# Chunk mask as four more features, score products in a row, and a regrouped output projection in a two-layer attention and convolution encoder

## The chip, the cores and the metric

One core of one Trainium2 chip. The metric is the time of one execution on the device, in microseconds (us). It was measured three times before the change.

## What is computed

Two layers work on 512 tokens of 1024 features in float32. Each layer adds half a SwiGLU network, then a mixing block, then half of another SwiGLU network, and normalises. The mixing block is what the change touches:

```python
h  = RMSNorm(x);  p = h @ W_in
# group A: 8 heads of latent attention; a head has 64 + 32 features of q and k, 64 of v
scores = einsum('bhqd,bhkd->bhqk', qs, ks) * scale      # 128 queries at a time
allowed = k_chunk <= q_chunk                            # chunks of 64 tokens
probs = softmax(where(allowed, scores, -1e30));  outs = probs @ vs
# group B: gated 512 channels, causal depthwise convolution over 31 tokens, layer norm, SiLU
x = x + concat(A, B) @ W_out                            # 512 + 512 rows
```

A block of 128 queries sees the keys up to its own end, so the mask matters only in the last 128 keys of a block: there the first 64 queries may not see the last 64 keys.

## The kernel before

Features lie on the 128 partitions and tokens along the free dimension, so an activation of 1024 features is eight blocks of 128 x 512. Large products are made of three fast ones each: operands are split into a high part of reduced precision and a low part that holds the rest, and `mm3` (L152 to L154) adds high x high, high x low and low x high. A weight block is 128 x 1024; `load_w` (L132) fetches it on SP's queue into `raw` (three buffers), ACT casts the high part into `wh` (L136), and the low part `wl` is made in one of three ways: by a subtraction on VectorE, by one on GpSimd (kinds named in `POOLW`; L142), or, for kind "sum", by a negated copy on ACT (L139) and a DMA on GpSimd's queue that adds the source (L140). `wh` and `wl` have four buffers each. PSUM has seven banks for `ps` and one called `cv`.

In `mix_body` the projections come first, in the order of `SEQ`. Queries (L711) and keys (L740) are made with tokens on the partitions, 96 features a head. Then each head runs through five stages, one behind another by the lags in `ORDER`: `turn` transposes q and k (L777, L782) and scales them (L779, L784); `scores` makes four score blocks of 128, 256, 384 and 512 keys (L800, contracted over 96 rows in two float32 passes), adds the mask to each by a bf16 product of `mrow` and `mneg` (L801), takes the largest (L802, VectorE) and the exponential (L806, ACT) of each; `turn_p` transposes the probabilities (L821) and copies them out (L824); `values` multiplies by v (L834); `turn_out` turns every pair of heads back (L852) and splits it (L159, L160) into one of the four blocks `at`. Blocks of 128 and 256 keys share a bank.

Beside the attention the convolution runs in the other engines: two of its four blocks wholly on VectorE (L888), two as products on ACT (L892) and additions on GpSimd (L896), `pr` in three buffers. Its four blocks `ys` are then summed on GpSimd (L910 to L912); a product with `onesm` gives the mean over channels (`pm`, L914); it is subtracted (L920), squares are taken and summed over channels by eight small products (L196), and `spread` (L215) broadcasts the scale. The four blocks `cv` come out of L930, L932 and the split.

The output projection has eight blocks of rows of its output. The weights of the first four (`WOP`) are loaded early, kind "sum", behind the keys; those of the last four when a buffer is free, kind "wo" (GpSimd). Three blocks (`WOG`) have their attention rows (k 0 to 3) multiplied early, between the steps of the convolution's norm; then come their convolution rows, then the next three blocks and the last two. Each result is added to x (L945).

The framework derives the waits between engines from the tiles, and orders each engine's instructions ahead of time with a simulated timeline, by the order in the program and by when operands are ready. Engines run their own instructions in that order. `tc.issue_after(i)` puts the instructions of a block behind instruction i on i's engine.

## Time and profile before

| | |
|---|---|
| three runs, us | 1805.57, 1805.58, 1807.63 |
| median, us | 1805.58 |
| the profiled execution, us | 1805.54 |
| its span in the profile, us | 1803.8 |
| granted TensorE clock | 0.999 |
| data moved | 226.23 MB, mean 125 GB/s |

PE is TensorE's products and PEld its weight loads, DVE is VectorE, POOL is GpSimd, SP issues loads. The span is the profiled execution from its first to its last instruction. In a row of the timeline the first number is the start and the second how long it took until the last of the merged instructions ended; a bracket tells how long the engine stood idle before, and who ended that. Products overlap one another in PE, so that start-to-start distances, not durations, tell what one costs.

### The profile page before, as it was taken

The page shows a single profiled execution, that of the slowest core. Times are in us where ns is not written, and L with a number is a line of the kernel's source. Part 1 is how long each engine was busy: PE and PEld are TensorE (multiplying, and loading weights), DVE is VectorE, ACT ScalarE, POOL GpSimd, SP SyncE. Part 2 cuts the span into 40 slices and gives each one's busy share as a digit, 9 for nine tenths or more (in the row PEclk, how much of TensorE's full clock was granted, in tenths as well). Part 3 has the DMA queues.
Part 4 walks back from the last instruction along what each step waited for, and adds up shares of the span by engine and source line. Part 5 has one row for each costly group of instructions (what it writes and reads, how often), then busy time and mean ns, then how long its engine had stood idle before and what let it go on. Part 6 is the DMA issues. An engine that isn't in the chain of part 4 may idle for free.

```text
span 1803.8 us, 30598 instructions
## 1 busy us (share of the span) xinstructions
PE 1786.7 (99%) x12198; PEld 1645.8 (91%) x12198; DVE 1423.3 (79%) x1975; ACT 1088.8 (60%) x1685; POOL 422.2 (23%) x343
## 2 busy tenths in 40 slices
PE   9999999999999999999999999999999999999998
PEld 7899999888788899999888999998978788999997
DVE  7888887588956979887779888866999668888873
ACT  5565656457953565656635656554779535656564
POOL 1000000258843000000310000002589410000001
PEclk9999999999999999999999999999999999999999
DMA  5657574324102466664326575743250126575742
GB/s 172 165 132 193 123 187 112 108 88 135 31 24 99 126 163 162 151 163 126 123 65 170 122 195 121 194 110 110 80 147 6 52 79 167 129 189 126 187 112 73
DMA packets 70415, 226.23 MB, mean 125 GB/s; under 512 B 7936, under 2 KB 8320, under 8 KB 70272
## 3 DMA queue, kind: packets, MB, share of 16 engines
q1 hardware_dynamic: 54000, 169.74, 28.1%
q0 software_dynamic: 16128, 54.53, 17.7%
q8 instruction: 95, 1.56, 0.4%
q14 instruction: 48, 0.39, 0.1%
q10 hardware_dynamic: 144, 0.00, 0.0%
HBM read 222.15 MB, written 2.10 MB: 124 GB/s over the span
## 4 chain that ended last, share of the span: by engine, by line
PE 80%; DVE 8%; ACT 5%; POOL 3%; issue 3%; DMA 1%; SPq 0%; ACTq 0%; POOLq 0%; DVEq 0%
PE ps L154 26%; PE ps L152 25%; PE ps L153 25%; POOL y L896 2%; PE ps L834 1%; DVE wl L244 1%; ACT pr L892 1%; DVE x L449 1%; DVE r L160 1%; ACT r L806 1%; PE ps L800 1%; DVE wl L142 1%; DVE cv L888 1%; DMA raw<-in_wgu 1%; ACT wh L136 1%
## 5 line engine op out<-in xcount | busy, mean ns | idle before, releaser
L153 PE MATMUL ps<-r,wh 128*128 128x256 f32 (+1 forms) x3436 | 1062.3, 309 | 0.1
L152 PE MATMUL ps<-r,wh 128*128 128x256 f32 (+1 forms) x3436 | 1061.0, 311 | 0.6 <-ACT r L159 0.3
L154 PE MATMUL ps<-r,wl 128*128 128x256 f32 (+1 forms) x2668 | 845.6, 318 | 2.6 <-DVE wl L142 1.2
L152 PEld LDWEIGHTS ps<-r,wh 128*128 128x128 f32 x3436 | 650.9, 190 | 38.6 <-ACT wh L136 2.1
L153 PEld LDWEIGHTS ps<-r,wh 128*128 128x128 f32 x3436 | 652.3, 190 | 36.4 <-issue 2.4
L154 PEld LDWEIGHTS ps<-r,wl 128*128 128x128 f32 x2668 | 506.9, 190 | 41.3 <-DVE wl L142 3.0
L136 ACT CAST wh<-raw 128x1024 fp32r<-128x1024 f32 (+3 forms) x148 | 132.1, 900 | 211.0 <-issue 101.3
L367 POOL DMA_DIRECT2D ls<-in_wgu x72 | 62.5, 869 | 741.7 <-ACT ls L366 615.3
L242 ACT CAST wh<-fr 128x1024 fp32r<-128x1024 f32 (+1 forms) x160 | 157.6, 985 | 101.5 <-DVE fr L387 39.7
L142 DVE TENSOR_TENSOR wl<-raw,wh 128x1024 fp32r<-128x1024 f32 (+3 forms) x132 | 146.8, 1117 | 91.0 <-ACT wh L136 90.0
L154 PE MATMUL ps<-r,ls 128*128 128x256 f32 x768 | 216.7, 282 | 0.0
L244 DVE TENSOR_TENSOR wl<-fr,wh 128x1024 fp32r<-128x1024 f32 (+1 forms) x160 | 182.9, 1143 | 40.3 <-ACT wh L242 40.3
L896 POOL TENSOR_TENSOR y<-y,pr 128x511 f32<-128x511 f32 (+14 forms) x120 | 157.4, 1312 | 54.6 <-ACT pr L892 47.4
L154 PEld LDWEIGHTS ps<-r,ls 128*128 128x128 f32 x768 | 145.2, 189 | 0.0
L244 DVE TENSOR_TENSOR wl<-raw,wh 128x1024 fp32r<-128x1024 f32 (+1 forms) x100 | 113.7, 1137 | 24.6 <-ACT wh L242 24.1
L189 POOL TENSOR_TENSOR r<-r,t 128x512 f32<-128x512 f32 x45 | 77.4, 1728 | 172.7 <-ACT t L185 171.9
L242 ACT CAST wh<-raw 128x1024 fp32r<-128x1024 f32 (+1 forms) x100 | 97.9, 979 | 27.9 <-PE ps L153 19.9
L366 ACT ACTIVATE ls<-fr 128x1024 fp32r<-128x1024 f32 (+1 forms) x56 | 56.1, 1002 | 78.6 <-PE ps L154 65.2
L892 ACT ACTIVATE pr<-r,vec 128x511 f32<-128x511 f32 (+14 forms) x120 | 85.3, 735 | 10.1 <-POOL y L896 10.1
L888 DVE SCALAR_TENSOR_TENSOR cv<-r,vec,cv 128x511 f32<-128x511 f32 (+14 forms) x120 | 88.0, 733 | 3.4 <-ACT cv L884 2.1
L449 DVE SCALAR_TENSOR_TENSOR x<-ps,x 128x512 f32<-128x512 f32 x112 | 77.1, 689 | 15.8 <-PE ps L154 15.4
L367 POOL DMA_DIRECT2D ls<-in_wdq x32 | 27.6, 863 | 260.5 <-ACT ls L366 260.5
(220 smaller groups left out, 2441.5 us busy)
## 6 DMA issues: line engine op xcount, KB each, us to landing
fr<-in_wgu SPq DMA_DIRECT2D x112, 512.0 KB, 3.4
ls<-in_wgu POOLq DMA_DIRECT2D x72, 512.0 KB, 6.3
raw<-in_wgu SPq DMA_DIRECT2D x62, 512.0 KB, 5.0
fr<-in_wdq SPq DMA_DIRECT2D x48, 384.0 KB, 4.6
ls<-in_wdq POOLq DMA_DIRECT2D x32, 384.0 KB, 4.7
raw<-in_wd SPq DMA_DIRECT2D x32, 384.0 KB, 3.1
raw<-in_wd SPq DMA_DIRECT2D x32, 256.0 KB, 2.7
raw<-in_wcv SPq DMA_DIRECT2D x16, 512.0 KB, 3.2
```

Of the source, the lines that this page charges most:

```text
L136: order["cast"] = A.copy(hi[:, :w], raw[:, :w]).ins
L142: (G if kind in POOLW.split() else V).tensor_tensor(lo[:, :w], raw[:, :w], hi[:, :w].bitcast(FP), ALU.subtract)
L152: T.matmul(o, lh, rh, start=first, stop=False, skip_group_check=free)
L153: T.matmul(o, lh, rl, start=False, stop=False, skip_group_check=free)
L154: order["mm"] = T.matmul(o, ll, rh, start=False, stop=last, skip_group_check=free).ins
L242: A.copy(hi[:, :w], src[:, :w])
L244: order["lo"] = V.tensor_tensor(lo[:, :w], src[:, :w], hi[:, :w].bitcast(FP), ALU.subtract).ins
L367: G.dma_start(out=lo[:, :n], in_=w, accum_op=ALU.add)
L449: return V.scalar_tensor_tensor(v, o.rearrange("p (m t) -> p m t", m=2), 0.5 * sign, v, ALU.mult, ALU.add).ins
L888: V.scalar_tensor_tensor(acc[:, s:], u[c][:, :S - s], tap(k), acc[:, s:], ALU.mult, ALU.add)
L892: A.activation(pr[:, s:], u[c][:, :S - s], AF.Copy, scale=tap(k))
L896: order["conv"] = G.tensor_tensor(acc[:, s:], acc[:, s:], pr[:, s:], ALU.add).ins
```

## The change

- q and k of a head get four more features (`DM` = 100). Feature i belongs to the i-th block of 128 tokens. In q it is 1 for the first 64 tokens of that block, in k it is -1e30 for the last 64 tokens; all else is 0. The values stand in 32 new columns of `consts`, and `mask_columns` writes them on GpSimd. The score product adds the mask itself; the products of `mrow` and `mneg` are gone.
- In `scores` the four products of a head are issued first, then the four reductions and exponentials.
- The output projection takes its weights as two blocks of output to one buffer, first (k 0 to 3) or second half (k 4 to 7) of the rows. The first halves of six blocks are loaded, kind "sum", behind the exponentials of heads 0, 2 and 4; their products run early: blocks 0 and 1 with k 0 to 2 ahead of the last `turn_out`, the rest between the steps of the norm. The second halves are loaded with the low part on VectorE; the last two blocks as before, kind "wo".
- The sum over `ys` runs on VectorE, block 2 last. The mean comes from a product with `ones`, and 1/512 goes into a fused subtraction. Mean, sums and scale of the norm use the bank `cv` instead of `ps`.
- Switches that are no longer used are removed.

```diff
+DM = DQ + 4
+WOH = (0, 2, 4)
...
+        def mask_columns(v, o):
+            G.tensor_tensor(v[:, :, :, DQ:DM], cst[:, o:o + 16].rearrange("p (t i) -> p t i", t=NT)[:, :, None, :]
+                            .to_broadcast([P, NT, H, 4]), ones.rearrange("p (t h i) -> p t h i", t=NT, h=H), ALU.mult)
...
-            for i in range(NT):
-                n = (i + 1) * P
-                o = (b01[:, 0:128], b01[:, 128:384], b2[:, 0:384], b3)[i]
-                T.matmul(o, qT[0:DQ, i * P:(i + 1) * P], kT[0:DQ, 0:n], start=True, stop=False)
-                heads[h]["s"] = T.matmul(o[:, n - 64:n], mrow, mneg, start=False, stop=True).ins
+            os = b01[:, 0:128], b01[:, 128:384], b2[:, 0:384], b3
+            for i, o in enumerate(os):
+                heads[h]["s"] = T.matmul(o, qT[0:DM, i * P:(i + 1) * P], kT[0:DM, 0:(i + 1) * P], start=True,
+                                         stop=True).ins
+            for i, (o, p) in enumerate(zip(os, ps)):
                 V.tensor_reduce(mx[:, i:i + 1], o, axis=AX.X, op=ALU.max, negate=True)
...
+        def load_wo(half, m, kind=""):
+            w = load_w(wout[l, m:m + 2, :, half * S:(half + 1) * S].rearrange("m p k -> p m k"), WC, kind, 2)
+            for i in range(2):
+                wo[half, m + i] = [v[:, i * S:(i + 1) * S] for v in w]
+        def products(ms, ks):
+            for k in ks:
+                for m in ms:
+                    if m not in early:
+                        early[m] = bank()
+                    w = wo[k // 4, m]
+                    c = slice(k % 4 * P, (k % 4 + 1) * P)
+                    mm3(early[m], w[0][:, c], w[1][:, c], *(at + cv)[k], k == 0, k == KD - 1)
...
+                if stage is turn_out and h == H - 1:
+                    for m, i in enumerate(WOH):
+                        with tc.issue_after(order["keys"]), tc.issue_after(heads[i]["e"]):
+                            load_wo(0, 2 * m, "sum")
+                    with tc.issue_after(order["values"]):
+                        products((0, 1), range(3))
...
-        with tc.issue_after(order["keys"]):
-            wo = [load_w(wout[l, m], WC, "sum") for m in range(WOP)]
...
+        with tc.issue_after(heads[H - 1]["s"]):
+            products((0, 1), range(3, 4))
         ysum = tmp()
-        G.tensor_tensor(ysum, ys[0], ys[1], ALU.add)
-        G.tensor_tensor(ysum, ysum, ys[2], ALU.add)
-        (G if YP else V).tensor_tensor(ysum, ysum, ys[3], ALU.add)
-        pm = bank()
-        T.matmul(pm, onesm, ysum, start=True, stop=True)
+        for a, b in ((ys[0], ys[1]), (ysum, ys[3]), (ysum, ys[2])):
+            V.tensor_tensor(ysum, a, b, ALU.add)
+        pm = own()
+        T.matmul(pm, ones, ysum, start=True, stop=True)
...
-        early_groups(range(E1, E2))
+        products((2, 3), range(4))
...
-            V.tensor_tensor(ys[c], ys[c], pm, ALU.subtract)
+            V.scalar_tensor_tensor(ys[c], pm, -1.0 / CW, ys[c], ALU.mult, ALU.add)
...
+        r = st.token(CW, own())
+        for m in (0, 2, 4):
+            load_wo(1, m)
+        products((4, 5), range(4))
+        pr = spread(r, own())
...
+        products(range(3), range(4, KD))
+        for m in range(3):
+            add(m)
+        for m in range(3, KD - 2):
+            products((m,), range(4, KD))
+            add(m)
+        ws = [load_w(wout[l, m], WC, "wo") for m in (KD - 2, KD - 1)]
+        for m, w in zip((KD - 2, KD - 1), ws):
+            early[m] = bank()
+            group(early[m], w, at + cv, range(KD), KD)
+            add(m)
```

## The prediction

> **What bounds the kernel now.** I read the page first, then the windows over one attention stage, then PE's timeline there, then its waits.

> ```profile
> span 1803.8 us, 30598 instructions
> PE 1786.7 (99%) x12198; PEld 1645.8 (91%) x12198; DVE 1423.3 (79%) x1975; ACT 1088.8 (60%) x1685; POOL 422.2 (23%) x343
> PEclk9999999999999999999999999999999999999999
> PE 80%; DVE 8%; ACT 5%; POOL 3%; issue 3%; DMA 1%; SPq 0%; ACTq 0%; POOLq 0%; DVEq 0%
> ```

> PE is busy 99% at full clock and holds 80% of the chain that ended last. So time is won only by taking instructions off PE or by closing places where PE stands still, and work of the other engines costs nothing until PE waits for it. The change touches two stretches of PE: the attention of each layer (about 450 to 508 and 1345 to 1401 us) and the output projection behind it. The windows, columns PE, PEld, DVE, ACT, POOL:

> ```profile
> 455.00:460.00 5.00, 3.62 (x21) 2.49 (x22) 4.87 (x11) 5.00 (x15) 4.51 (x5) 1.00 0.86 173
> 480.00:485.00 5.00, 5.00 (x40) 4.29 (x39) 4.89 (x10) 5.00 (x14) 4.69 (x5) 1.00 0.01 2
> 505.00:510.00 5.00, 4.22 (x32) 3.56 (x30) 1.66 (x3) 1.46 (x3) 2.83 (x3) 1.00 0.01 3
> ```

> At the start of attention PE works 3.62 of 5 us and ACT all 5; in its middle PE is full (ACT and DVE nearly so); at its end all wait for one another. These are the three places to price.

> **Mask.** Sixteen heads of four score products lose one mask product each, 64 in all. Dense PE of layer 0:

> ```profile
> L801 PE MATMUL ps<-mneg,mrow x64: 193/194/195, 451.0 to 1390.7; 128*128 128x64 bf16 x64
> 453.65 0.39 PE L800 MATMUL ps<-r,r 96*128 96x128 f32 x2
> 453.87 0.19 PE L801 MATMUL ps<-mneg,mrow 128*128 128x64 bf16 x1
> 453.90 0.89 PE L800 MATMUL ps<-r,r 96*128 96x384 f32 x2
> 454.63 0.19 PE L801 MATMUL ps<-mneg,mrow 128*128 128x64 bf16 x1
> 455.96 0.70 PE L800 MATMUL ps<-r,r 96*128 96x256 f32 x2 [1.14 <-ACT r L806]
> 456.49 0.19 PE L801 MATMUL ps<-mneg,mrow 128*128 128x64 bf16 x1
> 457.11 1.12 PE L800 MATMUL ps<-r,r 96*128 96x512 f32 x2 [0.42 <-ACT r L806]
> 458.07 0.19 PE L801 MATMUL ps<-mneg,mrow 128*128 128x64 bf16 x1
> 458.10 0.62 PE L777 MATMUL ps<-cst,q 128*96 128x128 f32 x4
> 458.55 0.60 PE L782 MATMUL ps<-cst,kn 128*96 128x128 f32 x4
> 458.99 0.39 PE L800 MATMUL ps<-r,r 96*128 96x128 f32 x2
> ```

> PE's durations overlap, so I price by starts. The two passes of the 128-wide score take 0.22 us (453.65 to 453.87), so 384 columns should take 0.66; with the mask before them they take 0.03 + 0.73 (453.87 to 454.63). A mask ahead of a score costs about 0.11. Ahead of eight transposes (458.07 to 458.99, 0.92 against eight of 0.11) it costs about 0.05. Going through the timeline, 36 masks stand ahead of a score and 28 ahead of something else: 36 x 0.11 + 28 x 0.05 = 5.4 us. Bounds: 64 x 0.03 = 1.9 (only the mask's own start-to-start) and 64 x 0.11 = 7.0. I take 4.5, because about a third of the masks lie where PE waits for ACT anyway.

> [...]

> The replacement adds no PE instruction: scores contract over 100 rows instead of 96 and stream the same columns; transposes have 100 columns of weights instead of 96, in a load that hides behind the previous product. Bounds 0 to 0.5 us (4% of 128 loads of about 0.1); I take 0. The four mask-column writes on POOL (two a layer, 128 elements a partition) are nearest to the table writes and sit beside idle POOL:

> ```profile
> 425.44 1.16 POOL L657 TENSOR_TENSOR tab<-cst,rg 128x64 f32<-128x64 f32 x4
> 421.59 3.88 POOL L171 TENSOR_TENSOR scq<-ssh,minus_half 128x8 f32<-128x8 f32 x1 [2.75 <-DVE ssh L716]
> ```

> About 0.3 to 0.6 us each; POOL waits 2.75 us for DVE right there, so nothing, or up to 0.6 a layer if they land ahead of a root that PE's transposes need.

> **Scores in a row.** In the rows above, the 256-wide score shares its bank with the 128-wide one and starts only after that one's exponential: 455.96 - 454.63 - 0.03 = 1.30 us of PE. Issued before any reduction, it can't wait for it, and its bank is given back sooner. The like gaps behind masks in layer 0 (457.11; 460.88, 464.11, 468.68 in the timeline) are 0.59, 0.26, 0.49 and 0.55, together 3.2; in layer 1 1.5 (0.32, 0.26, 0.47, 0.49). All end with ACT's exponential. Of 4.7 I count 1.5: the first, and little else, because ACT is full there and its conv taps stay. The price is that the first reduction of a head waits for one more product (0.43 us), with a stage of lead to hide it.

> **Output projection.** PE's holes, what ends the convolution, and the wait of layer 1 before its last transposes (the row without a time, from the view of waits):

> ```profile
> 499.00 5.08 POOL L896 TENSOR_TENSOR y<-y,pr 128x485 f32<-128x485 f32 x4
> 504.04 1.26 POOL L910 TENSOR_TENSOR t<-r,y 128x512 f32<-128x512 f32 x1
> 506.72 1.26 POOL L912 TENSOR_TENSOR t<-t,r 128x512 f32<-128x512 f32 x1
> 505.29 2.34 PE L834 MATMUL ps<-r,r 128*128 128x64 f32 x20
> 508.42 0.66 PE L852 MATMUL ps<-cst,t 128*128 128x128 f32 x4 [0.78 <-DVE t L841]
> 508.91 1.02 PE L914 MATMUL ps<-t,onesm 128*128 128x512 f32 x2
> 522.28 0.39 PE L154 MATMUL ps<-r,wl 128*128 128x512 f32 x1
> 522.85 1.19 PE L152 MATMUL ps<-r,wh 128*128 128x512 f32 x4 [0.17 <-ACT r L159]
> 534.30 0.39 PE L152 MATMUL ps<-r,wh 128*128 128x512 f32 x1
> 534.53 0.39 PE L153 MATMUL ps<-r,wh 128*128 128x512 f32 x1
> 535.15 0.50 PE L154 MATMUL ps<-r,wl 128*128 128x512 f32 x1 [0.23 <-POOL wl L142]
> 1402.29 1.13 PE L914 MATMUL ps<-t,onesm 128*128 128x512 f32 x2 [0.34 <-POOL t L912]
> PE ps L852 <- DVE t L841: 0.8, 1, 0.8
> 512.72 2.28 DVE L189 TENSOR_TENSOR r<-r,t 128x512 f32<-128x512 f32 x3
> ```

> A dense product starts every 0.23 (534.30 to 534.53). Holes of layer 0: 0.89 before the last transposes (505.29 + 20 x 0.112 = 507.53), 0.34 for the first conv rows, 0.39 for a low weight part: 1.6. Layer 1 has the same three (0.94, 0.33 and 0.40 by starts) and 0.56 at the conv mean: 2.2. Sum 3.8.

> Afterwards 72 early products stand ready instead of 48 (in the timeline a fourth block's first rows already ran ahead, 519 to 522). At 0.23, with the mean, the four sums, the spread and the last transposes (about 3 us), that is 19.5 us of PE work. The conv chain: POOL's last add ends at 504.1, and before the change three sums of 1.26 follow on POOL. Now two of them are done by then and the third runs on DVE, 0.76 (2.28 for three); the mean could start at 505 instead of 508.9. From mean to first conv rows it took 522.85 - 508.91 = 13.9, so they are there at 519. PE leaves the values at about 504.5 and has work to 524: 5 us to spare. The hole before the last transposes is filled by the 18 products issued ahead of them. So the holes close; I keep 0.8 back for new ones and count 3.0.

> What is moved must fit into that spare time. Eight loads a layer had eight casts (ACT), four negated copies (ACT), four accumulating DMAs and four subtractions (POOL); now eight, three, three, three subtractions on DVE and two on POOL:

> ```profile
> 452.98 1.05 ACT L139 ACTIVATE wl<-raw 128x1024 fp32r<-128x1024 f32 x1
> 453.93 1.03 ACT L136 CAST wh<-raw 128x1024 fp32r<-128x1024 f32 x1
> 455.46 0.35 ACT L806 ACTIVATE r<-ps,mx 128x128 f32<-128x128 f32 x1
> L142 DVE TENSOR_TENSOR wl<-raw,wh x132: 681/1058/2833, 15.6 to 1776.4; 128x1024 fp32r<-128x1024 f32 x56, 128x768 fp32r<-128x768 f32 x38, 128x512 fp32r<-128x512 f32 x32, 128x864 fp32r<-128x864 f32 x4
> L142 POOL TENSOR_TENSOR wl<-raw,wh x8: 2407/2853/2867, 532.7 to 1435.9; 128x1024 fp32r<-128x1024 f32 x8
> ```

> The second half of blocks 2 and 3 may be cast once blocks 0 and 1 are through their first rows (about 510), ready by 514; that of 4 and 5 some 5.4 us later; they are needed from 524. These casts and subtractions wait for PE, and behind them in the ACT and DVE queues stand squares, scaling and SiLU of the conv chain, for which PE waits next: 3 x (1.04 + 1.06 to 2.83) us at the worst, against 5 spare. The last two blocks get buffers at about 524 and 532 and need 1.04 + 2.9 us; their turn is at 540. Loads on SP are ahead by three raw buffers, with the same bytes in half as long runs, so a slower landing is hidden too; without that lead PE would wait out the landing once. One POOL issue (about 1 us) fewer lets the conv adds go on. The mean by an unscaled matrix and a fused subtraction costs DVE at most 0.05 x 4, on the spared chain.

> **Sum.** 4.5 + 1.5 + 3.0 - 0.5 (strides, POOL columns, a later first reduction) = 8.5 us. The profiled execution took 1805.54 (span 1803.8 and 1.7 around it), next to the median 1805.58: 1797.0. Own range: most 7.0 + 4.7 + 3.8 = 15.5 (1790), least 1.9 + 0 + 2.0 = 3.9 (1801.6).

> **Rivals.**
> 1. *ACT binds the attention.* It shows 5.00 of 5 in two windows. PE's shorter heads then wait for exponentials, and only the projection gains: 2 to 3 us, less what sticks, 1802 to 1805. Against: in the full middle stretch PE stood still nowhere though ACT was full, because ACT's slots hold conv taps that can move back; the conv chain has 5 us to give. Chance 0.20.
> 2. *Slower: the preloads in ACT's queue.* Three cast-and-negate pairs now go behind the exponentials of heads 0, 2 and 4, in the fullest part, 2.1 us each. The pair at 452.98 stands right ahead of the exponential at 455.46 for which PE waited until 455.96. If all of it turned into PE waits, 6 x 2.1 = 12.6, the start's 1.5 is lost and 7.5 gained: 5 us slower, about 1810. It decides from 60% of that ACT time becoming PE time. Against: one pair fewer, and two of the old four lay as near. Chance 0.12.
> 3. *The mask is worth only its own start, or is given back.* 1.9 instead of 4.5: 1799.6. Chance 0.08.

> **Chances.** Forecast 0.60, rivals 0.20, 0.12, 0.08. A measurement tells 0.2% (3.6 us) from no change. Faster: 0.60 + 0.08 and a fifth of rival 1, 0.72; the rest of that rival is the same, 0.16; slower 0.12. The range leaves out rival 2 and a little below: 1790.5 to 1805.

> **What would show it.** No bf16 products on PE; score passes of 384 columns 0.66 us a pair; the 256-wide score right behind the 128-wide one; PE without a hole between the values of the last head and the first conv rows; the conv mean within 1.5 us of POOL's last add; 72 products ahead of the conv rows. Wrong would be new PE waits for the exponentials in the first three heads, for DVE or ACT weight parts at 515 to 545 us of the old clock, or a conv mean queued on PE ahead of ready products and waiting for POOL.

## The result: slower by 0.35%, and the profile after

| | before | after |
|---|---|---|
| median, us | 1806.80 (7 runs) | 1813.38 (7 runs, 1812.0 to 1814.35) |
| the profiled execution, us | 1805.54 | 1814.0 |
| its span, us | 1803.8 | 1812.2 |
| granted TensorE clock | 0.999 | 0.997 |

The ratio is 1.0035, 95% interval [1.0023, 1.0047]: slower by 6.6 us where 8.5 us faster had been forecast. The head of the page after, with its row of granted clocks:

```profile
span 1812.2 us, 30466 instructions
PE 1787.8 (99%) x12134; PEld 1646.0 (91%) x12134; DVE 1426.9 (79%) x1982; ACT 1087.9 (60%) x1683; POOL 406.8 (22%) x335
PEclk9999999999999999999999999999999999999999
```

PE has 64 instructions fewer and yet 1.1 us more busy time, so some of its instructions ran slower. Forty slices of 45 us are too coarse to see which. The windows are finer (columns PE, PEld, DVE, ACT, POOL, granted clock):

```profile
455.00:460.00 5.00, 3.53 (x14) 2.00 (x13) 5.00 (x11) 4.64 (x11) 4.69 (x5) 0.85 0.00 0
460.00:465.00 5.00, 4.37 (x17) 2.30 (x15) 4.62 (x10) 5.00 (x14) 4.34 (x5) 0.81 0.53 131
1370.00:1377.00 7.00, 7.00 (x26) 5.66 (x26) 4.69 (x9) 5.59 (x15) 6.50 (x6) 0.52 0.42 75
463.00:473.00 10.00, 7.35 (x46) 5.10 (x44) 10.00 (x21) 10.00 (x25) 7.57 (x7) 1.00 0.46 105
```

The change's record of the clock holds two values over these stages, 1.0 and 0.5; 0.85 and 0.81 over two windows of 5 us are (0.15 + 0.19) x 5 / 0.5 = 3.4 us at half clock, and the row of layer 1 holds 6.7 us of it. In the profile of before the clock is whole from 5 us until PE's last product at 1797 us. The mean clocks of single executions tell what that is worth: the change took 1812.0 and 1812.3 us at 0.999 and 1.000 and 1813.0 to 1814.4 at 0.995 to 0.997, and the kernel before, in its 29 executions beside run 1, 1805.2 to 1806.4 at 0.998 or 0.999 and 1807.2 to 1810.3 in the seven at 0.995 to 0.998. So half clock added some 2 us to an execution of either kernel, and the change is about 6 us slower where neither has it, as far as these means can be trusted (one, 0.948 in run 8, stands beside an ordinary time). The fourth row shows a loss of the other kind: at full clock PE works 7.35 of 10 us, with ACT and DVE full. ACT's timeline says what it does there, and PE's who waits:

```profile
454.05 0.70 ACT L901 ACTIVATE pr<-r,vec 128x484 f32<-128x484 f32 x1 [0.60 <-POOL y L905]
455.36 0.70 ACT L901 ACTIVATE pr<-r,vec 128x483 f32<-128x483 f32 x1 [0.60 <-POOL y L905]
455.96 0.35 ACT L795 ACTIVATE r<-ps,mx 128x128 f32<-128x128 f32 x1
457.44 0.68 ACT L795 ACTIVATE r<-ps,mx 128x512 f32<-128x512 f32 x1
458.68 1.05 ACT L123 CAST wh<-raw 128x1024 fp32r<-128x1024 f32 x1
459.61 1.07 ACT L126 ACTIVATE wl<-raw 128x1024 fp32r<-128x1024 f32 x1
460.57 0.48 ACT L795 ACTIVATE r<-ps,mx 128x256 f32<-128x256 f32 x1
```

```profile
451.18 2.32 PE L791 MATMUL ps<-r,r 100*128 100x128 f32 x8
457.02 1.12 PE L791 MATMUL ps<-r,r 100*128 100x512 f32 x2 [1.34 <-ACT r L795]
459.87 3.72 PE L791 MATMUL ps<-r,r 100*128 100x128 f32 x8
464.60 1.01 PE L809 MATMUL ps<-cst,r 128*128 128x128 f32 x6 [0.57 <-ACT r L795]
467.25 2.32 PE L791 MATMUL ps<-r,r 100*128 100x128 f32 x8
471.85 0.44 PE L809 MATMUL ps<-cst,r 128*128 128x128 f32 x2 [1.36 <-ACT r L795]
1357.62 1.88 PE L791 MATMUL ps<-r,r 100*128 100x384 f32 x4 [1.54 <-ACT r L795]
```

The pair of 2.1 us (cast L123, negated copy L126) stands ahead of the last of head 0's four exponentials (a head has one of each width, and the 256-wide one comes last here), and the next pair stands likewise right before the wait at 471.85. In layer 1 the wait of 1.54 us follows its pair too (1354.52 to 1356.53). The wait of 1.34 us at 457.02, ahead of the first half-clock stretch, doesn't: it is older than the first pair. There the exponentials began late, at 455.96, because two of the convolution's products on ACT (taps, L901) ahead of them waited 0.60 us each for POOL to give back a `pr` buffer. Run 14 below has the same two waits and run 9 has neither, so they too come with the place of the loads, by way of the order in ACT's queue. The four score products of a head, eight passes in a row, take 2.32 us at full clock and 3.72 us where about half of them fall into the slow stretch. Behind the attention, the chain of the convolution's norm came late:

```profile
503.80 3.78 POOL L905 TENSOR_TENSOR y<-y,pr 128x484 f32<-128x484 f32 x3 [0.48 <-ACT pr L901]
511.75 0.69 DVE L829 TENSOR_TENSOR t<-ps,rs 128x512 f32<-128x512 f32 x1 [0.87 <-PE ps L822]
513.87 0.69 DVE L913 TENSOR_TENSOR t<-t,y 128x512 f32<-128x512 f32 x1
518.48 1.02 PE L918 MATMUL cv<-t,ones 128*128 128x512 f32 x2
528.68 0.95 PE L183 MATMUL cv<-ones,r 128*128 128x1 f32 x8
531.91 1.02 PE L202 MATMUL cv<-t,ones 128*128 128x512 f32 x2
531.34 0.50 PE L139 MATMUL ps<-r,wh 128*128 128x512 f32 x1 [0.90 <-ACT wh L123]
533.93 0.50 PE L141 MATMUL ps<-r,wl 128*128 128x512 f32 x1 [0.99 <-POOL wl L129]
```

POOL ends the convolution at 507.6, but the sum over its blocks (L913) stands in DVE's queue behind the last head's scaling (L829), which waits for PE. Mean, sums and spread (L918, L183, L202) then each stand in PE's queue behind products that are ready. PE runs out of those at 531 and takes up block 6, whose weights aren't there.

One measure is used here for the two layers' attention (440 to 500 and 1336 to 1400 us) and the projection behind it (to 545 and 1445). For each PE product it takes the distance to the next start less the median distance of that shape, and adds them up. It counts standstill and slow passes alike. A shape is the rows, columns and type of a product.

| us lost by PE | attention, layers 0 and 1 | projection, layers 0 and 1 | sum |
|---|---|---|---|
| before | 4.4, 3.4 | 2.8, 3.5 | 14.0 |
| after | 10.5, 9.7 | 3.3, 3.4 | 26.8 |
| run 9 (below) | 3.7, 2.5 | 2.6, 2.6 | 11.4 |

The change lost 12.8 us more in these places, nearly all in the attention, and the span grew by 8.4. That leaves about 4.4 us for the work taken off PE (in run 9, by the same count, 5.2 - 2.6 = 2.6), and far more than that was lost again. The measure is coarse: with products grouped also by what stands before or after them the 12.8 becomes anything from 12 to 15.5.

### The profile page after: what moved, and what is told of

Read it like the earlier page. It is cut to its first block, busy times and chain, and to the rows that moved or that the text cites. A ratio compares the mean times of both kernels' runs of the same rounds, so it can differ in the third digit from the quotient of the medians.

```text
span 1812.2 us, 30466 instructions
## 1 busy us (share of the span) xinstructions
PE 1787.8 (99%) x12134; PEld 1646.0 (91%) x12134; DVE 1426.9 (79%) x1982; ACT 1087.9 (60%) x1683; POOL 406.8 (22%) x335
## 5 line engine op out<-in xcount | busy, mean ns | idle before, releaser
L139 PE MATMUL ps<-r,wh 128*128 128x256 f32 (+1 forms) x3436 | 1057.9, 311 | 2.6 <-ACT wh L123 1.8
L139 PEld LDWEIGHTS ps<-r,wh 128*128 128x128 f32 x3436 | 651.2, 190 | 39.7 <-ACT wh L123 4.1
L123 ACT CAST wh<-raw 128x1024 fp32r<-128x1024 f32 (+3 forms) x148 | 132.1, 900 | 193.2 <-issue 92.9
L129 DVE TENSOR_TENSOR wl<-raw,wh 128x1024 fp32r<-128x1024 f32 (+3 forms) x138 | 153.9, 1121 | 83.6 <-ACT wh L123 82.8
L905 POOL TENSOR_TENSOR y<-y,pr 128x511 f32<-128x511 f32 (+14 forms) x120 | 159.8, 1336 | 54.0 <-ACT pr L901 46.6
L901 ACT ACTIVATE pr<-r,vec 128x511 f32<-128x511 f32 (+14 forms) x120 | 85.3, 740 | 14.8 <-POOL y L905 14.7
```

The costliest lines, as they stand in the source:

```text
L123: order["cast"] = A.copy(hi[:, :w], raw[:, :w]).ins
L129: (G if kind in POOLW.split() else V).tensor_tensor(lo[:, :w], raw[:, :w], hi[:, :w].bitcast(FP), ALU.subtract)
L139: T.matmul(o, lh, rh, start=first, stop=False, skip_group_check=free)
L901: A.activation(pr[:, s:], u[c][:, :S - s], AF.Copy, scale=tap(k))
L905: order["conv"] = G.tensor_tensor(acc[:, s:], acc[:, s:], pr[:, s:], ALU.add).ins
```

## The experiments

The runs are numbered 1 to 14 by their names e1 to e14. Each was compared with the kernel before on the same chip, whose median was 1805.8 to 1806.3 us.

**Run 1, the mask alone.** The kernel before with the mask features; the mean by `ones` with a fused subtraction makes room for them.

```diff
-                T.matmul(o, qT[0:DQ, i * P:(i + 1) * P], kT[0:DQ, 0:n], start=True, stop=False)
-                heads[h]["s"] = T.matmul(o[:, n - 64:n], mrow, mneg, start=False, stop=True).ins
+                heads[h]["s"] = T.matmul(o, qT[0:DM, i * P:(i + 1) * P], kT[0:DM, 0:n], start=True, stop=True).ins
```

> Only the mask as four more features is put into the kernel before (and the mean by an unscaled matrix with a fused subtraction, for room); scores stay one product, one reduction, one exponential after another, the projection stays. Theory L (the early weight loads in ACT's queue among the exponentials make PE wait) and theory R (the row of products makes the exponentials late) both expect this to be faster by what the mask costs, 3 to 5 us. Theory M (with shorter heads PE runs into ACT, stands, and its clock is halved) expects no gain or a loss up to 5 us, with a granted clock below 1.00 in a window of the attention's start.

Measured 1806.59 us, ratio 1.0003 [0.9994, 1.0011]. PE's timeline of this run, three rows that have a wait:

```profile
456.40 0.70 PE L800 MATMUL ps<-r,r 100*128 100x256 f32 x2 [1.55 <-ACT r L805]
508.54 1.12 PE L913 MATMUL ps<-t,ones 128*128 128x512 f32 x2 [0.47 <-POOL t L911]
1401.87 2.02 PE L913 MATMUL ps<-t,ones 128*128 128x512 f32 x2 [1.78 <-POOL t L911]
```

No change: the first two theories fell. The work is gone from PE, and PE gets to the exponentials and to the conv mean earlier than these. The mean of layer 1 also ran at half clock (2.02 us instead of 1.12; 0.50 from 1402 to 1404 us); at the start of attention, where theory M had it, the clock stayed whole.

**Run 2, scores in a row alone.**

```diff
-            for i in range(NT):
+            os = b01[:, 0:128], b01[:, 128:384], b2[:, 0:384], b3
+            for i, o in enumerate(os):
...
+            for i, o in enumerate(os):
                 V.tensor_reduce(mx[:, i:i + 1], o, axis=AX.X, op=ALU.max, negate=True)
```

> Only the order in scores is changed in the kernel before: four products with their mask products, then four reductions and exponentials. Theory R expects 4 to 8 us slower, with new PE waits for exponentials in the first three heads. Theory L expects between 2 us faster (the 1.3 us wait of the 256-wide product goes) and no change; theory M no change.

Measured 1805.86 us, 0.9996 [0.9987, 1.0004].

```profile
457.25 1.12 PE L800 MATMUL ps<-r,r 96*128 96x512 f32 x2 [1.20 <-ACT r L805]
461.61 1.12 PE L800 MATMUL ps<-r,r 96*128 96x512 f32 x2 [0.75 <-ACT r L805]
```

The wait of the 256-wide product is gone and stands, about as long, at the 512-wide one. Theory R fell.

**Run 3, the projection alone**, with the early loads behind the exponentials as in the change, but with mask products and interleaved scores.

> Only the regrouped projection is put into the kernel before, with its three early loads behind the exponentials of heads 0, 2 and 4; mask by bf16 products and scores one after another as before. Theory L expects 5 to 10 us slower, nearly the whole loss of the change and the mask's 5 us on top, with casts and negated copies ahead of the exponentials PE waits for. Theories R and M expect 0 to 4 us faster, from the holes of the projection.

Measured 1818.0 us, 1.0066 [1.0053, 1.0079]: worse than all three parts together, and worse than the theory of the loads had it. The profiled execution is the slowest of the six (1823.2 us).

```profile
474.00:478.00 4.00, 4.00 (x23) 3.82 (x22) 3.86 (x6) 4.00 (x11) 3.68 (x3) 0.58 0.77 146
1372.00:1389.00 17.00, 17.00 (x71) 14.08 (x71) 10.27 (x19) 12.81 (x27) 11.68 (x10) 0.51 0.33 68
```

The windows show nearly 17 us in one piece at half clock. The loss is in the attention, where this kernel differs from the one before only in its loads.

**Run 4, the change with its early loads behind the keys.** One line:

```diff
-                        with tc.issue_after(order["keys"]), tc.issue_after(heads[i]["e"]):
+                        with tc.issue_after(order["keys"]):
```

> The changed kernel with its three early loads behind the keys only, as in the kernel before, so that casts and negated copies lie before the attention. Theory L expects 8 us or more below the changed kernel, so 2 to 6 us faster than the kernel before, clock 1.00 throughout. Theories R and M expect it within 2 us of the changed kernel, 5 to 8 us slower than the kernel before.

Measured 1806.04 us, 0.9997 [0.9988, 1.0006]: 7.3 us below the change (6.5 if each is set against its own kernel before) and equal to before. So the place of six loads (three a layer), with the order that the schedule makes of it, accounts for the whole slowdown, and the forecast gain is still missing. What remains:

```profile
453.89 1.03 ACT L123 CAST wh<-raw 128x1024 fp32r<-128x1024 f32 x1
457.31 0.70 ACT L901 ACTIVATE pr<-r,vec 128x484 f32<-128x484 f32 x1 [0.84 <-POOL y L905]
457.91 0.56 ACT L795 ACTIVATE r<-ps,mx 128x384 f32<-128x384 f32 x1
458.62 2.08 PE L791 MATMUL ps<-r,r 100*128 100x512 f32 x2 [2.43 <-ACT r L795]
527.04 0.50 PE L139 MATMUL ps<-r,wh 128*128 128x512 f32 x1 [0.90 <-ACT wh L123]
529.62 0.50 PE L141 MATMUL ps<-r,wl 128*128 128x512 f32 x1 [1.00 <-POOL wl L129]
```

A cast of a second half has gone ahead into the first exponentials, since its buffer is free. A convolution tap (L901) waits for POOL to give back a `pr` buffer, and the exponential behind it waits too. PE stands still for 2.43 us and goes on at half clock (2.08 us for a product of 1.12; 0.62 over 458 to 460 us). The two waits for block 6's weights are still there.

**Runs 5 and 6, the sum over the convolution on VectorE.** Run 1, and run 1 with scores in a row, with the sum as the change has it:

```diff
-        G.tensor_tensor(ysum, ys[0], ys[1], ALU.add)
-        G.tensor_tensor(ysum, ysum, ys[2], ALU.add)
-        (G if YP else V).tensor_tensor(ysum, ysum, ys[3], ALU.add)
+        for a, b in ((ys[0], ys[1]), (ysum, ys[3]), (ysum, ys[2])):
+            V.tensor_tensor(ysum, a, b, ALU.add)
```

> The mask-only kernel with the sum over the four conv blocks on VectorE instead of GpSimd. In the mask-only run PE reached the conv mean earlier and stood there for GpSimd's sum (0.63 us in layer 0, 1.94 in layer 1, then 3.4 us at half clock). Theory G (the mask's gain was given back at the conv mean, because GpSimd's chain did not move) expects the wait at the mean gone and 3 to 5 us less than the kernel before. The rival, that the gain was given back at the attention's start to ACT, expects within 1.5 us of the kernel before.

> The same with the four score products in a row. If the row only moves the start's waits from one product to another, as the row-only run shows (3.5 us against 3.2), it is within 1.5 us of the run without the row. If the row gains its own 1.5 us once PE is no longer held at the mean, it is 1 to 3 us faster than that.

Measured 1811.5 us (1.0028 [1.0017, 1.004]) and 1808.83 us (1.0017 [1.0008, 1.0025]). I had thought that VectorE would have the sum sooner; that theory fell, and so did its rival, which had no change. PE's row for the mean in run 5:

```profile
511.61 1.57 PE L912 MATMUL ps<-t,ones 128*128 128x512 f32 x2 [2.09 <-DVE t L910]
```

The sum waits in DVE's queue for the last head, as in the change, and with no early products placed before the mean PE stands still. The clock behind it is halved in both layers (0.51 and 0.50, the windows under run 10). Run 6 is 2.7 us faster than run 5, as the row's own gain would have had it, but its profile has no half clock at the start of attention, where run 5's has 6.8 us; so this isn't shown to be the row's gain.

**Run 7, mean and sums ahead of the ready products** (run 4, with the products of blocks 0 to 3 held back until the mean, those of 4 and 5 until the sums).

> The changed kernel with early loads behind the keys, and on PE the conv mean ahead of the last quarter of blocks 0 and 1 and of blocks 2 and 3, the norm's sums ahead of blocks 4 and 5. Theory Q (the conv norm's steps are late because PE's queue puts ready products ahead of them: the mean 3.9 us and the sums 4.5 us after their operands) expects the conv rows 4 to 6 us earlier, the waits of 1.07 and 1.16 us for block 6's weights gone from both layers, 3 to 6 us faster than the run with early loads. The rival, that block 6's weights are late in themselves, expects the same two waits and no change.

Measured 1806.05 us, 1.0000 [0.9991, 1.0009]. Mean and sums came early, but the spread (L203) still stood behind the products of blocks 4 and 5: it came 1.9 us earlier than in run 4 (525.7 against 527.6), the convolution's rows only 0.4 us earlier, and block 6's low part was waited for, as long as its two waits in run 4 together:

```profile
529.19 0.50 PE L141 MATMUL ps<-r,wl 128*128 128x512 f32 x1 [1.72 <-POOL wl L129]
```

**Run 8, run 4 with the low part of the last two blocks on VectorE** (`load_w(wout[l, m], WC)` without "wo").

> The changed kernel with early loads behind the keys, and the low part of the last two blocks on VectorE (1.06 us) instead of GpSimd (2.4). Theory Q expects the 1.16 us wait to shrink to 0.2 or less and the 1.07 us wait for the cast to stay: 1 to 2 us faster than the run with early loads. The rival expects the waits to go to the next step of the norm instead, no change.

Measured 1805.61 us, 0.9997 [0.9988, 1.0006]: the wait for POOL went, the 0.90 for the cast stayed, and 0.42 for a conv row came. POOL wasn't the cause of the late tail.

**Run 9, order and loads together.** Run 4 with the order of run 7, the spread also taken ahead and the second halves cast behind the last exponential:

```diff
+        with tc.issue_after(order["mean"]):
+            products((0, 1), range(3, 4))
+            products((2, 3), range(3))
...
+        with tc.issue_after(heads[H - 1]["e"]):
+            for m in (0, 2, 4):
+                load_wo(1, m)
+        with tc.issue_after(st.last):
+            products((2, 3), range(3, 4))
+            products((4, 5), range(1))
+        pr = spread(r, own(), order)
+        with tc.issue_after(order["spread"]):
+            products((4, 5), range(1, 4))
```

> The changed kernel with the first loads of the output projection behind the keys (as in the fourth run), and now with the order around the conv norm written out for TensorE: mean, the rest of blocks 0 and 1 and most of 2 and 3, sums, block 3's rest and one product group of 4 and 5, spread, the rest of 4 and 5; the casts of the second halves stand behind the last exponential. Theory queue order (what the projection was to give, 3.0 us, is lost because the norm's short steps stand behind ready products and a cast stands among the first exponentials): the two waits of 1.07 and 1.16 us a layer for block 6's weights go, spread comes out by about 524 instead of 527.6, and the first score wait shrinks by the 1.1 us of one cast: 4 to 6 us below the fourth run's 1806.0, so 1800 to 1802. Rival, another wait takes their place (the conv rows' SiLU on ScalarE, or the eviction of block 0): 1805 to 1806.5, with a PE wait of 1 us or more between 525 and 545 us.

Measured 1800.33 us, 0.9965 [0.9953, 0.9978]: 6.0 us faster than the kernel before and about 13 us faster than the change.

One of its windows, and then PE's timeline:

```profile
455.00:460.00 5.00, 4.74 (x21) 2.51 (x19) 5.00 (x11) 5.00 (x15) 4.74 (x4) 1.00 0.00 0
```

```profile
509.42 1.02 PE L917 MATMUL cv<-t,ones 128*128 128x512 f32 x2
515.76 0.94 PE L183 MATMUL cv<-ones,r 128*128 128x1 f32 x8
521.06 1.10 PE L203 MATMUL cv<-t,ones 128*128 128x512 f32 x2 [1.48 <-DVE t L199]
```

PE works 4.74 of the 5 us that had 3.62 before and 3.53 after; the clock is whole throughout (mean 0.999); the spread runs at 521 instead of 532, and neither wait for block 6's weights is left. A new wait of 1.48 us for the spread's operand took part of that.

**Run 10, the clock by itself.** Run 5 with eight products into the mean's own bank, which the mean overwrites; the early products are held behind the mean, where run 5 had them too:

```diff
+        with tc.issue_after(order["back"]):
+            for _ in range(8):
+                T.matmul(pm, at[0][0][:, 0:P], at[0][0], start=True, stop=True)
...
+        with tc.issue_after(order["mean"]):
+            early_groups(range(E1))
...
```

> The fifth run (mask as features, sum over the convolution on VectorE; 1811.5 us) with eight products of 0.22 us into the mean's own bank ahead of the mean, which overwrites them; they lie in the 2.25 us in which TensorE waits at the mean. The order after the mean is the fifth run's. Theory clock gate (a wait of 2 us makes the granted clock fall to 0.5 for 3.4 us, which costs 1.7 us of products on top of the wait): no slices at 0.5 behind the mean (512.1 to 515.5, 1406.4 to 1409.8 before), and 2 x 1.7 = 3.4 us less, 1807.5 to 1808.5. Rival, the half clock has another cause than the wait (it follows from the load of the 60 us ahead of it): the same slices at 0.5 remain and the time is 1811 to 1812, or more if the fillers push the mean back.

Measured 1807.5 us, 1.0005 [0.9996, 1.0014], against 1811.5 of run 5. The same two windows of layer 0 and 1, first run 5, then run 10:

```profile
512.00:515.50 3.50, 3.50 (x8) 2.32 (x7) 2.29 (x4) 1.53 (x3) 0.00 (x0) 0.51 0.00 0
1406.40:1409.80 3.40, 3.14 (x6) 1.84 (x7) 1.17 (x3) 0.63 (x3) 0.00 (x0) 0.50 0.02 5
```

```profile
512.00:515.50 3.50, 3.50 (x17) 2.88 (x16) 3.29 (x7) 2.40 (x4) 0.00 (x0) 1.00 0.00 0
1406.40:1409.80 3.40, 3.40 (x17) 2.81 (x16) 3.19 (x6) 1.87 (x4) 0.00 (x0) 1.00 0.00 0
```

More work for PE made the kernel 4.0 us faster (4.5 against each one's own kernel before). With the wait filled the clock stayed whole (1.00 instead of 0.51 and 0.50), and the same 3.5 us then hold 17 instructions instead of 8. That the wait, not the load of the time before it, halved the clock is thereby shown for this place. Of the 4.0 us, 2 x 1.7 answer to these two stretches; the stretch at the start of attention was also shorter in run 10's profile (3.4 us against 6.8), which I didn't touch.

**Run 11, run 9 with run 8's edit.**

> The ninth run's kernel with the low part of the last two blocks' weights made on VectorE instead of GpSimd (the eighth run's edit). Theory queue order: with the spread early GpSimd is no longer late, so this changes nothing, within 1 us of the ninth run. Rival, GpSimd's place binds still: 1 to 2 us faster than the ninth run, because the wait for the low part of 1.16 us a layer is still there in the ninth and gone here.

Measured 1800.18 us, 0.9966 [0.9954, 0.9979]: no change from run 9.

**Run 12, run 9 with interleaved scores** (run 2's edit undone).

> The ninth run's kernel with the scores of a head as before the change: each product followed by its maximum and exponential in program order, not four products in a row. Theory that the row only moves the wait (as the second run had it, 1805.86 against 1805.97): within 1 us of the ninth run. Rival, with the mask gone from TensorE the row brings the start wait of 2.6 us on the 512-wide product with the half clock behind it: 2 to 4 us faster than the ninth run. Rival on the other side, the row brings its forecast 1.5 us: 1 to 2 us slower.

Measured 1801.18 us, 0.9970 [0.9958, 0.9981]: 0.85 us slower than run 9 in the medians. The rival that had it faster fell; the one that had it 1 to 2 us slower missed narrowly. The intervals overlap, but five of the six executions are above all five of run 9: a small gain of the row is likely, its size isn't resolved.

**Run 13, run 12 with the 64 mask products back.**

> The twelfth run's kernel (ordered projection, scores interleaved; 1801.2 us, 5.2 below before) with the mask again as 64 products of bf16 on TensorE instead of four features. Theory that the mask's own price was right and its gain was eaten by waits in the first run: 3.5 to 5 us slower than the twelfth run, 1804.5 to 1806. Rival, the mask's price was too high (a wait for ScalarE stands in its place even here) and the ordered projection holds the gain: within 1.5 us of the twelfth run, 1801 to 1802.7.

Measured 1804.66 us, 0.9992 [0.9983, 1.0001]. Against the kernel before on each one's own chip, run 12 has -5.15 us and run 13 -1.32: the mask features are worth 3.8 us where nothing waits behind them. The ordered projection has the remaining 1.3, which by itself can't be told from no change.

**Run 14, run 9 with the early loads back behind the exponentials** (run 4's line undone, nothing else).

> The ninth run's kernel (1800.3 us) with its three early loads each behind the last exponential of head 0, 2 and 4, as the change has them, and nothing else. Theory that the casts and negated low parts (2.1 us a pair) in ScalarE's queue between exponentials hold TensorE and halve its clock: 6 to 8 us slower than the ninth run, 1806 to 1808.5, with granted clock at 0.5 between 455 and 480 us. Rival, the loads cost only together with the second-half cast that the changed kernel has among its first exponentials and that the ninth run moved: 1 to 3 us slower, 1801 to 1803.5, and no half clock.

Measured 1810.82 us, 1.0027 [1.0016, 1.0038]: 10.5 us slower than run 9, more than either theory said. The timelines of ACT and PE, and two windows:

```profile
458.75 1.05 ACT L123 CAST wh<-raw 128x1024 fp32r<-128x1024 f32 x1
459.68 1.07 ACT L126 ACTIVATE wl<-raw 128x1024 fp32r<-128x1024 f32 x1
461.26 1.90 PE L792 MATMUL ps<-r,r 100*128 100x384 f32 x4 [1.04 <-ACT r L796]
471.94 0.44 PE L810 MATMUL ps<-cst,r 128*128 128x128 f32 x2 [1.36 <-ACT r L796]
```

```profile
472.00:481.50 9.50, 9.50 (x46) 8.16 (x47) 8.28 (x17) 8.74 (x23) 8.92 (x8) 0.64 0.49 109
1370.00:1375.50 5.50, 5.50 (x35) 5.42 (x35) 4.21 (x8) 5.50 (x15) 5.08 (x5) 0.69 0.75 160
```

The waits are those of the change again, each pair followed by one; and there are half-clock stretches of (0.36 x 9.5) / 0.5 = 6.8 us and (0.31 x 5.5) / 0.5 = 3.4 us, with a third at 463 to 467. As in the change, the first wait of run 14 (1.34 us at 457.08) is older than its first pair.

## Why the prediction was wrong

**Preloads in ACT's queue (rival 2, given 0.12).** This is the step that made the kernel slower: the sum put the preloads at nothing. It went as this rival says, at its place and mostly by its mechanism; only the first wait of layer 0 came ahead of the pairs, behind taps. The rival's threshold went by waits alone: 60% of 12.6 us of ACT time would have to become PE time. Runs 4 and 14 measured the place of the loads at 7.3 and 10.5 us (6.5 and 10.8 against each one's own kernel before), 52 to 86% of those 12.6. Some of it is half clock, which no term of the prediction had; most is waits, for executions with a mean clock of 0.999 or 1.000 took 1812.0 and 1812.3 us in the change and 1805.3 to 1806.6 in run 4. At the low end the forecast gain of the rest would have made up for it, but run 4 shows that the rest brought nothing. The argument against it ("one pair fewer, and two of the old four lay as near") counted pairs and not their place between exponentials. With the early loads behind the keys there are as many pairs, and the loss is gone (run 4). The sign that the prediction named for this, new PE waits for exponentials in the first three heads, is the one that came. That ACT's part of the loads costs this, and not their transfers, is read from the releasers of PE's waits; no run moved the one without the other.

**ACT can wait because its taps can move back (against rival 1).** This step failed. The taps stand in ACT's queue where the schedule put them; in run 4 one of them waits 0.84 us for POOL with an exponential behind it. ACT, busy for 60% of the change's span, had no room for an exponential that stood behind that tap.

**Mask, 4.5 us.** The mechanism and about the size were right: 3.8 us by runs 12 and 13. (By its own rows a mask ahead of a score costs 0.10 us, 0.03 + 0.07, and not 0.11.) Of it run 1 shows nothing, because PE then waits for ScalarE at the start and for POOL at the mean instead. The price by starts (0.11 and 0.05 us a mask) held better than the mask's own start-to-start (64 x 0.03 = 1.9 us), which rival 3 took: the runs show twice that. That a third of the masks lie where PE waits anyway was the right kind of doubt, but the whole was lost, not a third.

**Scores in a row, 1.5 us.** Mis-sized. Run 2 shows the wait of 1.14 us at the 256-wide product turn into one of 1.20 at the 512-wide one: ACT was the releaser of both, and freeing a bank gave ACT no time. Run 12 leaves it at 0.85, its size unresolved.

**Output projection, 3.0 us.** The step that failed is the conv chain, mean at 505 and conv rows at 519. I took POOL's last add for the last thing the mean waits for. After, the add ended at 507.6, the sum at 514.6 behind the last head's scaling in DVE's queue, and the mean ran at 518.5 behind ready products in PE's. The "5 us to spare" were thereby used up, and block 6 was needed too early. The 18 products ahead of the last transposes did close that hole. Ordered (run 13), the whole is worth 1.3 us instead of 3.0, with a wait for the spread's operand left (1.48 us in run 9).

**Clock.** PE's clock was read as full and left there. In the change's profile about 10 us ran at half clock (3.4 + 6.7), which is 5 us of PE work; as PE would have waited for ACT in part of it, less of that is lost time, some 2 us by the mean clocks of its executions. This is not the step that failed: executions of the change without it are slower than the kernel before as well.

**Sum.** With the two repairs of run 9 the three parts bring 1.3 + 3.8 + 0.85 = 6.0 us of the 8.5 that I had forecast (they are steps of one series of runs, so that they add up by construction; the 0.5 taken off for strides and columns was not tested); with the loads where the change has them, they lose that and as much again.

## What to carry to other kernels

When a change moves a load, follow every instruction that the load issues into the queue of the engine that runs it, and ask what stands behind it there; an engine that is 60% busy over the span can be full just in that stage (ACT, 5.00 of 5 us from 460 to 465 in the change). Work taken off the bounding engine is only worth something once the waits that it then reaches earlier are priced too; here one part alone gave nothing, and the order of a short dependent chain among ready products decided. Look at the granted clock in windows of a few microseconds: a wait of 2.1 us was followed by 3.4 us at half clock, which is 1.7 us of PE's work (run 5), and filling it with useful or even useless products may pay (run 10, 4.0 us).
